# Weight pieces in one tile, block inverses on GpSimd, and a swap of two subtractions in a one-core hybrid encoder step

## The chip, the cores and the metric

The kernel runs on one core of a Trainium2 chip. A core has a matrix engine (PE, with its weight loads shown apart as PEld), a vector engine (DVE), a scalar engine (ACT), GpSimd (POOL) and a queue engine (SP, SyncE) from which this kernel issues all of its DMAs; 16 DMA engines move the bytes. Each engine takes its own instructions strictly in the order in which they stand in the program, and waits on semaphores for the others.

The metric is the device time of one execution in microseconds (us). Times below are of the kernel before, and one execution of it was taken by the profiler.

## The reference

One layer of a streaming encoder is computed, for a prompt of 2048 tokens and for 64 frames of a running stream ("sample"), width 1024, 16 heads of 64 in four groups of four heads.

- `proj = x @ w_in` gives the inputs of four mixers. A is a gated delta rule (a short convolution, then chunks with a triangular solve), B is stick-breaking attention, C is an mLSTM, D is HGRN2.
- Each head's output is normalised, two groups are gated, and `mix = o @ w_out`.
- `x = LN(alpha*x + mix)`, then `x = LN(alpha*x + relu(x@w1+b1)^2 @ w2 + b2)` with a hidden width of 4096.
- The new states and the new keys and values are outputs too.

Two places matter here. In mixer A a chunk of 128 tokens solves with `eye + lm`, unit lower triangular:

```python
sol = lax.linalg.triangular_solve(eye + lm, rhs, left_side=True, lower=True, unit_diagonal=True)
```

In mixer B the weight of a key is `exp(log_sigmoid(z) + after)`, where `after` sums `log_sigmoid(-z)` over all later keys up to the query. The kernel therefore walks the keys backward in steps of 128 keys and carries the running sum from step to step.

## The kernel before

**Numbers in two pieces.** PE multiplies rounded numbers (type fp32r), so an operand is split into a rounded part `hi` and a rest `lo = x - hi`. Every product is three matmuls (`mm3`): in L468 and L469 and L470 of the profile stand hi by hi, and the two mixed products. A split takes a copy that rounds (mostly ACT) and a subtraction (DVE or POOL).

**The dense work.** The tokens are in four blocks of 512, and the 64 sample tokens ride along. `project` multiplies each block by `w_in`, one column group after the other; `mix` multiplies by `w_out`; `mlp` does the two MLP products, and it begins for the first block when the fourth block is projected. In `mlp`, `up` makes 256 hidden columns (ReLU and square on ACT in L1632 and L1633, the rounded copy into `hh` on DVE in L1634, the rest on DVE in L1638), and `down` multiplies them by `w2` and adds to an accumulator `acc` on DVE (L1653).

**Weights.** `load_w` fetches one weight tile (128 x 512 or 528 numbers) for the matmuls. At a weight's first use SP loads it raw (L459), ACT makes `whi` (L460), POOL makes `wlo` (L461), and SP stores both to scratch in HBM (`wsp`, L196). At each later use SP loads both pieces from `wsp` by two DMAs of 256 KB (L196). Each piece has a ring of six tiles. SP waits at a load until the tile's last readers are done, and all DMAs behind it wait too.

**The other work.** Four generators run beside the dense one: attention (`attention`, then `attention_sample`), the gates, the delta rule (`gdn`) and the two memories (`mlstm`, `hgrn`). `interleave` places their PE work between the dense matmuls by due times; the order of PE's instructions is thus fixed when the program is written. The order on DVE, ACT, POOL and SP is made by the scheduler of the language, which simulates the program while it is built; a tile of a ring is given out there when a slot is free.

**The inverses.** `gdn` runs nine times (two chunks at a time for the prompt, one for the sample). It needs the inverse of the 16 x 16 diagonal blocks of all chunks and heads. They lie with one block per partition (64 partitions) in `ub`; L960 to L971 compute the inverse in `wb` row by row on DVE: a negation, and 15 times a product (L965, up to 15 x 15 numbers per partition) and a sum (L971). Then the inverses go through HBM (`wd`) to other partitions, and PE uses them (L1000 and on). All of L960 to L971 is one chain in which each instruction needs the one before.

**One attention step.** PE makes scores two steps ahead (L1358, L1359). `stick` bounds them (DVE L1323) and takes softplus (ACT L1288, L1289). `add_carry` adds the carry to one row (DVE L1298) and splits the result: ACT L1300 and the rest on POOL in L1301. PE sums over keys (L1308 with the rounded part, L1309 with the rest) into `c`. `weights` subtracts (DVE L1315), takes exp (ACT L1316), and splits: ACT L1318, and the rest on DVE in L1319. PE multiplies by the values (`add_up`: L1368 with the rounded part, L1369 with the rest), which stands on PE one step later, behind the sums of the next step. The carry of the next step comes from `c`. There are 160 such steps for the prompt and 17 for the sample.

Of the kernel before, what the change touches and what calls it, by code (L numbers as in the profile page):

```python
# [13 lines left out]
P = 128  # L14
D = 1024
# [15 lines left out]
R_AS, R_AR, R_AQ, R_AK, R_OB = 5, 4, 3, 6, 1  # L31
# [7 lines left out]
R_G2, R_G1, R_H2, R_H1 = 10, 9, 3, 12  # L39
# [17 lines left out]
def encoder_step(ctx: ExitStack, tc: tile.TileContext, a, o):  # L57
# [131 lines left out]
    pd = psring(psd, "d")  # L189

# [251 lines left out]
    def load_w(w, r0, k, c0, n, end=False):  # L442
# [129 lines left out]
    def into_place(b):  # L572

        ld = []
        for t in b.tiles:
            ld.append(bp.tile([P, 4 * UNIT], F32, tag="acc", name=nm("acc"), bufs=R_ACC)[:, :D])
            SP.dma_start(ld[-1][: t.n], t.x)
        if not b.i:
            yield 0, 4
        for j, t in enumerate(b.tiles):  # L580
            if b.i:
                yield from need("xfree", b.i, j)
            yield from put_T(t, t.off, [ld[j][:, 512 * g : 512 * g + 512] for g in range(2)])
# [284 lines left out]
    def gdn(u):  # L868
# [91 lines left out]
        DVE.tensor_scalar(ub[:PB], ub[:PB], -1.0, None, ALU.mult)  # L960
        fill_in(wb[:PB], 0.0)
        POOL.memset(wb[:PB].rearrange("p r c -> p (r c)")[:, ::17], 1.0)
        for i in range(14, -1, -1):
            m = 15 - i
            DVE.tensor_tensor(  # L965
                tb[:PB, :m, :m],
                wb[:PB, i + 1 :, i + 1 :].rearrange("p j c -> p c j"),
                ub[:PB, i, i + 1 :].unsqueeze(1).to_broadcast([PB, m, m]),
                ALU.mult,
            )  # L970
            DVE.tensor_reduce(wb[:PB, i, i + 1 :], tb[:PB, :m, :m], axis=AX.X, op=ALU.add)  # L971
# [320 lines left out]
    def add_carry(sp, carry):  # L1292
# [8 lines left out]
        POOL.tensor_tensor(sl, sp, sh.bitcast(F32), ALU.subtract)  # L1301
# [10 lines left out]
    def weights(zc, c):  # L1312
# [6 lines left out]
        DVE.tensor_tensor(al, zc, ah.bitcast(F32), ALU.subtract)  # L1319
# [175 lines left out]
    def bcast_row(src):  # L1495
        x = bp.tile([P, 4 * UNIT], F32, tag="brd", name=nm("brd"), bufs=R_BRD)[:, :D]
        SP.dma_start(x, src.partition_broadcast(P))
        return x
# [56 lines left out]
    def mix(ts_, ld):  # L1555

        for t in ts_:
            t.acc = bp.tile([P, 4 * UNIT], F32, tag="acc", name=nm("acc"), bufs=R_ACC)[: t.n, :D]
# [32 lines left out]
        for t in ts_:  # L1591
            POOL.tensor_tensor(t.acc, t.acc, bb1[: t.n], ALU.add)
            SP.dma_start(t.x1, t.acc)

# [244 lines left out]
```

## Time and profile before

| | us |
|---|---|
| runs (median of 3; lowest to highest) | 3465.78 (3459.81 to 3467.36) |
| the profiled execution, its own time | 3468.76 |
| its span, first to last instruction | 3466.7 |
| PE busy | 3160.0 (91%) |
| DVE busy | 2275.2 (66%) |
| ACT busy | 1342.0 (39%) |
| POOL busy | 860.7 (25%) |
| mean granted TensorE clock | 0.952 |

The page gives one execution. Busy times count instructions of the engine, not the waits of its sequencer, and not the issuing of DMAs. A row of a view by lines reads: line, engine, operation, output and inputs by the program's names, shape, count, then busy time and the mean of one, then the idle time of the engine just before these instructions and what ended it. The span of 3466.7 us and the own time of 3468.76 us differ by 2.06 us that lie around the instructions.

### The profile page before, as it was taken

How to read it: one execution, taken by the hardware profiler on the slowest of the kernel's cores; microseconds unless marked ns; L12 is line 12 of the kernel's file. 1: busy time of each engine (PE TensorE's matmuls, PEld its weight loads, DVE VectorE, ACT ScalarE, POOL GpSimd, SP SyncE). 2: the span in 40 equal slices, each digit the busy share in tenths (PEclk: the TensorE clock that was granted, in tenths of full speed). 3: DMA queues.
4: the chain of work that ended last, by engine and by line, in shares of the span. 5: the costliest groups of instructions: out<-in, count | busy, mean ns of one | idle time of the engine just before them, and what ended most of it. 6: DMA issues, size and time to landing. Idle time of an engine off the chain costs nothing.

```text
span 3466.7 us, 60038 instructions
## 1 busy us (share of the span) xinstructions
PE 3160.0 (91%) x20906; PEld 2686.4 (77%) x20906; DVE 2275.2 (66%) x5360; ACT 1342.0 (39%) x3048; POOL 860.7 (25%) x946
## 2 busy tenths in 40 slices
PE   6987799999889878988988987999999999999998
PEld 6977788878777667776766766888887888898987
DVE  2656556558757887888889889757556354564445
ACT  2433343425446346556556555444212111121111
POOL 3432112113124233455354453121101000010001
PEclk9998899999989889999988988999999999999999
DMA  7985666676567676665765875657787576765542
GB/s 236 304 267 177 185 213 187 201 212 196 175 207 232 202 250 191 204 220 189 249 223 187 268 204 167 197 163 240 247 279 261 187 265 235 263 228 161 167 159 88
DMA packets 573882, 735.62 MB, mean 212 GB/s; under 512 B 104472, under 2 KB 300748, under 8 KB 573580
## 3 DMA queue, kind: packets, MB, share of 16 engines
q1 hardware_dynamic: 573580, 731.79, 65.9%
q8 instruction: 166, 2.72, 0.3%
q14 instruction: 136, 1.11, 0.1%
HBM read 548.63 MB, written 182.94 MB: 211 GB/s over the span
## 4 chain that ended last, share of the span: by engine, by line
PE 43%; DVE 10%; DMA 2%; issue 1%; ACT 1%; SPq 1%; POOL 1%; POOLq 0%; DVEq 0%; ACTq 0%
PE d L468 13%; PE d L469 12%; PE d L470 12%; DVE acc L1653 1%; DVE g L890 1%; PE d L531 1%; DVE ar L1319 1%; DVE as L1315 0%; DVE g L965 0%; PE po L1369 0%; DVE as L1298 0%; PE a L1309 0%; SPq L196 0%; PE a L1358 0%; PE a L1308 0%
## 5 line engine op out<-in xcount | busy, mean ns | idle before, releaser
L468 PE MATMUL d<-XH,whi 128*128 128x512 f32 (+1 forms) x1840 | 678.6, 369 | 19.4 <-ACT whi L460 8.5
L469 PE MATMUL d<-XL,whi 128*128 128x512 f32 (+1 forms) x1840 | 662.1, 360 | 0.8 <-DVE XL L484 0.8
L470 PE MATMUL d<-XH,wlo 128*128 128x512 f32 (+1 forms) x1840 | 660.5, 359 | 1.2 <-DMA wlo<-wsp 0.7
L1653 DVE TENSOR_TENSOR acc<-d,acc 128x512 f32<-128x512 f32 x564 | 386.0, 687 | 251.5 <-PE d L470 239.3
L468 PE MATMUL d<-whi,hh 128*128 128x512 f32 x992 | 405.4, 409 | 8.0 <-ACT x L1632 2.8
L468 PEld LDWEIGHTS d<-XH,whi 128*128 128x128 f32 x1840 | 352.8, 192 | 69.2 <-ACT whi L460 8.7
L469 PE MATMUL d<-wlo,hh 128*128 128x512 f32 x992 | 397.7, 401 | 5.3 <-POOL wlo L461 5.2
L1301 POOL TENSOR_TENSOR ar<-as,ar 128x512 fp32r<-128x512 f32 (+3 forms) x177 | 210.0, 1186 | 753.5 <-ACT ar L1300 617.0
L470 PE MATMUL d<-whi,hh 128*128 128x512 f32 x992 | 396.6, 400 | 0.0
L470 PEld LDWEIGHTS d<-XH,wlo 128*128 128x128 f32 x1840 | 352.1, 191 | 53.4 <-DMA wlo<-wsp 1.1
L469 PEld LDWEIGHTS d<-XL,whi 128*128 128x128 f32 x1840 | 353.0, 192 | 45.6 <-DVE XL L484 1.5
L1632 ACT ACTIVATE x<-d,cbig 128x512 f32<-128x512 f32 (+1 forms) x160 | 97.8, 611 | 677.9 <-PE d L470 659.5
L461 POOL TENSOR_TENSOR wlo<-raw,whi 128x512 fp32r<-128x512 f32 (+1 forms) x204 | 276.2, 1365 | 299.4 <-ACT whi L460 199.7
L468 PE MATMUL d<-whi,XH 128*128 128x256 f32 (+1 forms) x1024 | 307.2, 300 | 15.9 <-DMA whi<-wsp 10.4
L469 PE MATMUL d<-wlo,XH 128*128 128x256 f32 (+1 forms) x1024 | 301.2, 294 | 17.9 <-DMA wlo<-wsp 11.0
L470 PE MATMUL d<-whi,XL 128*128 128x256 f32 (+1 forms) x1024 | 297.9, 291 | 1.2 <-DVE XL L484 1.1
L1634 DVE CAST hh<-x 128x512 fp32r<-128x512 f32 (+1 forms) x160 | 75.3, 471 | 272.3 <-ACT x L1633 272.1
L468 PEld LDWEIGHTS d<-whi,hh 128*128 128x128 f32 x992 | 190.6, 192 | 54.1 <-ACT x L1632 3.2
L469 PEld LDWEIGHTS d<-wlo,hh 128*128 128x128 f32 x992 | 190.9, 192 | 46.9 <-POOL wlo L461 5.5
L470 PEld LDWEIGHTS d<-whi,hh 128*128 128x128 f32 x992 | 190.5, 192 | 45.1
L469 PEld LDWEIGHTS d<-wlo,XH 128*128 128x128 f32 x1024 | 203.2, 198 | 23.8 <-DMA wlo<-wsp 14.7
L468 PEld LDWEIGHTS d<-whi,XH 128*128 128x128 f32 x1024 | 203.6, 199 | 22.5 <-DMA whi<-wsp 12.3
(439 smaller groups left out, 6352.2 us busy)
## 6 DMA issues: line engine op xcount, KB each, us to landing
whi<-wsp SPq DMA_DIRECT2D x644, 256.0 KB
wlo<-wsp SPq DMA_DIRECT2D x644, 256.0 KB
wsp<-whi SPq DMA_DIRECT2D x196, 256.0 KB
wsp<-wlo SPq DMA_DIRECT2D x196, 256.0 KB
raw<-in_w_dram SPq DMA_DIRECT2D x128, 256.0 KB
acc<-in_x_prompt_dram SPq DMA_DIRECT2D x32, 512.0 KB
raw<-in_w_in_dram SPq DMA_DIRECT2D x52, 256.0 KB
ak<-kk SPq DMA_DIRECT2D x80, 128.0 KB
```

The costliest lines, as they stand in the source:

```text
L461: POOL.tensor_tensor(lo, raw, hi.bitcast(F32), ALU.subtract)
L468: PE.matmul(out, lhsT=lh, rhs=rh, start=start, stop=False)
L469: PE.matmul(out, lhsT=lh, rhs=rl, start=False, stop=False)
L470: PE.matmul(out, lhsT=ll, rhs=rh, start=False, stop=stop)
L531: PE.matmul(pt, lhsT=lhs(k), rhs=r, start=k == ks[0] and i == 0, stop=k == ks[-1] and i == 1)
L890: DVE.scalar_tensor_tensor(dst[:, i], xin[:, i, j : j + N], convw(2 * p + i, j), dst[:, i], ALU.mult, ALU.add)
L1301: POOL.tensor_tensor(sl, sp, sh.bitcast(F32), ALU.subtract)
L1319: DVE.tensor_tensor(al, zc, ah.bitcast(F32), ALU.subtract)
L1632: ACT.activation(r, pt, AF.Relu, bias=b1c(ff))
L1634: DVE.tensor_copy(h[:, f, cs], r)
L1653: lambda pt, first, acc=acc: DVE.tensor_tensor(acc, pt, acc, ALU.add),
```

## The change

- **Weights.** `hi` and `lo` of a weight lie side by side in one tile `wt` with one ring of six, and in one scratch tensor. A first use stores both by one DMA, and a later use loads both by one DMA of 512 KB instead of two of 256 KB. Only the last 8 weights of the last MLP, whose pieces go into 16 tiles of other rings, are still fetched by two DMAs.
- **Inverses.** The negation on DVE goes. Column after column, for 15 columns, POOL now does a product and a subtraction of at most 64 numbers per partition, where DVE did a product and a sum.
- **Attention.** The rest in `add_carry` goes from POOL to DVE, and the rest in `weights` from DVE to POOL.
- **MLP.** The rounded copy into `hh` goes from DVE to ACT.
- **Tiles.** The accumulators (`acc`, 6), the broadcast rows (`brd`, 2) and the hidden tiles (`hh`, 2) are no longer rings whose slots the scheduler gives out: each is one fixed tile, cut into parts that the program takes by turn or from a list of free ones. Two rings get one tile less: `ak` (keys and values of attention, 6 to 5) and `g2` (tiles of `gdn`, 10 to 9).

PE's instructions and their order stay as they are, but for two neighbours that change places at the start.

```diff
-R_AS, R_AR, R_AQ, R_AK, R_OB = 5, 4, 3, 6, 1
+R_AS, R_AR, R_AQ, R_AK, R_OB = 5, 4, 3, 5, 1
...
-R_G2, R_G1, R_H2, R_H1 = 10, 9, 3, 12
+R_G2, R_G1, R_H2, R_H1 = 9, 9, 3, 12
...
+    accs = bp.tile([P, R_ACC, 4 * UNIT], F32, name="acc")
+    acc_free = list(range(R_ACC))
+
+    def acc_take(o):
+        o.acc_i = acc_free.pop(0)
+        o.acc = accs[: o.n, o.acc_i, :D]
+
+    def acc_give(o):
+        acc_free.append(o.acc_i)
+
+    brd_ = fixed("brd", 4 * UNIT, R_BRD)
+    hh_ = fixed("hh", -(-SB // P * 2 * BN // UNIT) * UNIT, R_HH, F32R)
...
-            hi, lo = (wp.tile([P, 2 * UNIT], F32R, tag=tag, name=nm(tag), bufs=W_SP)[:, :m] for tag in ("whi", "wlo"))
+            both = wp.tile([P, 4 * UNIT], F32R, tag="wt", name=nm("wt"), bufs=W_SP)[:, : 2 * m]
+            hi, lo = both[:, :m], both[:, m:]
         key = (w.tensor.name, r0, c0)
-        if key in split:
-            for x, d in zip((hi, lo), split[key]):
-                move(x, d)
-        else:
+        if key not in split:
...
-            split[key] = [dram([P, m], F32, "wsp") for _ in range(2)]
-            for x, d in zip((hi, lo), split[key]):
-                move(d, x)
+            split[key] = dram([P, 2 * m], F32, "wsp")
+            move(split[key], both)
+        elif end:
+            move(hi, split[key][:, :m])
+            move(lo, split[key][:, m:])
+        else:
+            move(both, split[key])
...
-        DVE.tensor_scalar(ub[:PB], ub[:PB], -1.0, None, ALU.mult)
         fill_in(wb[:PB], 0.0)
         POOL.memset(wb[:PB].rearrange("p r c -> p (r c)")[:, ::17], 1.0)
-        for i in range(14, -1, -1):
-            m = 15 - i
-            DVE.tensor_tensor(
-                tb[:PB, :m, :m],
-                wb[:PB, i + 1 :, i + 1 :].rearrange("p j c -> p c j"),
-                ub[:PB, i, i + 1 :].unsqueeze(1).to_broadcast([PB, m, m]),
-                ALU.mult,
-            )
-            DVE.tensor_reduce(wb[:PB, i, i + 1 :], tb[:PB, :m, :m], axis=AX.X, op=ALU.add)
+
+        for j in range(15, 0, -1):
+            up_ = [PB, j, 16 - j]
+            POOL.tensor_tensor(tb[:PB, :j, : 16 - j], bc(ub[:PB, :j, j], up_), wb[:PB, j, j:].unsqueeze(1).to_broadcast(up_), ALU.mult)
+            POOL.tensor_tensor(wb[:PB, :j, j:], wb[:PB, :j, j:], tb[:PB, :j, : 16 - j], ALU.subtract)
         DVE.tensor_copy(tb[:PB], wb[:PB].rearrange("p r c -> p c r"))
...
-        POOL.tensor_tensor(sl, sp, sh.bitcast(F32), ALU.subtract)
+        DVE.tensor_tensor(sl, sp, sh.bitcast(F32), ALU.subtract)
...
-        DVE.tensor_tensor(al, zc, ah.bitcast(F32), ALU.subtract)
+        POOL.tensor_tensor(al, zc, ah.bitcast(F32), ALU.subtract)
...
-                    DVE.tensor_copy(h[:, f, cs], r)
+                    ACT.copy(h[:, f, cs], r)
```

The order of the instructions shows three places. The line numbers of the changed kernel differ: there L483 is the raw load, L485 the rest of a weight, L222 the moves, L989 the last fill ahead of the inverse, L993 and L994 the inverse, L1321 the carry's row, L1324 the rest in `add_carry`, L1338 the subtraction in `weights`, L1342 the rest in `weights`.

POOL, at the fourth call of `gdn` (first chunks of the second block), before: L962 is the last fill ahead of the inverse, and L994 there is the masking that follows the inverse.

```order
L962 MEMSET g_2320_12363 64x16
L1138 TENSOR_TENSOR h_2343_12530<-h_2277_12164,cbig 128x256
L1301 TENSOR_TENSOR ar_12545<-as_12349,ar_12544 128x512
L200 MEMSET h_2357_12627 128x512
L200 MEMSET h_2359_12633 128x4
L994 TENSOR_TENSOR g_2324_12433<-g_2164_11518,cbig 64x256 x2
```

The same place on POOL in the changed kernel, cut in the fourth column of 15:

```order
L989 MEMSET g_2059_11918 64x16
L993 TENSOR_TENSOR g_2060_11919<-g_2058_11917,g_2059_11918 64x15
L994 TENSOR_TENSOR g_2059_11918<-g_2059_11918,g_2060_11919 64x15
L993 TENSOR_TENSOR g_2060_11919<-g_2058_11917,g_2059_11918 64x14x2
L994 TENSOR_TENSOR g_2059_11918<-g_2059_11918,g_2060_11919 64x14x2
L993 TENSOR_TENSOR g_2060_11919<-g_2058_11917,g_2059_11918 64x13x3
L994 TENSOR_TENSOR g_2059_11918<-g_2059_11918,g_2060_11919 64x13x3
L1161 TENSOR_TENSOR h_2078_12076<-h_2016_11719,cbig 128x256
L993 TENSOR_TENSOR g_2060_11919<-g_2058_11917,g_2059_11918 64x12x4
L1342 TENSOR_TENSOR ar_12086<-as_11769,ar_12085 128x512
```

Thirty instructions of the inverse now stand on POOL, and attention's rest of the weights (L1342) stands among them; 21 more of them follow before the next L1342.

DVE at the same call, before: the inverse (L960, L965, L971) stands among the steps of the memories (L1127 to L1132) and of attention (L1315, L1298, L1319).

```order
L960 TENSOR_SCALAR g_2319_12362<-g_2319_12362 64x256
L1127 COPY cbig<-h_12505 128x4
L965 TENSOR_TENSOR g_2321_12364<-g_2320_12363,g_2319_12362 64x1
L1128 SCALAR_TENSOR_TENSOR cbig<-cbig 128x4
L1315 TENSOR_TENSOR as_12214<-as_12214,a_12532 128x512
L1298 TENSOR_TENSOR as_12349<-as_12349,a_12532 1x512
L971 TENSOR_REDUCE g_2320_12363<-g_2321_12364 64x1
L1129 TENSOR_TENSOR cbig<-cbig 128x4
L965 TENSOR_TENSOR g_2321_12364<-g_2320_12363,g_2319_12362 64x2x2
```

The same attention step on DVE in the changed kernel:

```order
L1150 COPY cbig<-h_12051 128x4
L1151 SCALAR_TENSOR_TENSOR cbig<-cbig 128x4
L1338 TENSOR_TENSOR as_11769<-as_11769,a_12078 128x512
L1152 TENSOR_TENSOR cbig<-cbig 128x4
L1321 TENSOR_TENSOR as_11904<-as_11904,a_12078 1x512
L1153 RECIPROCAL cbig<-cbig 128x4
L1155 TENSOR_TENSOR h_2077_12062<-h_12051,cbig 128x256
L1157 TENSOR_TENSOR h_2077_12062<-h_2077_12062,h_2018_11724 128x256
L1324 TENSOR_TENSOR ar_12091<-as_11904,ar_12090 128x512
```

The inverse has left DVE, and the rest of the sums (L1324) stands where the rest of the weights (L1319) stood some rows later.

SP soon after the start, before: raw loads, stores of single pieces, and L1707, which clears scratch.

```order
L459 DMA raw_410<-in_w_in_dram 128x2x256
L196 DMA wsp_385<-wlo_379 128x512
L459 DMA raw_702<-in_w_in_dram 128x2x256
L196 DMA wsp_395<-wlo_389 128x512
L1707 DMA wd_370<-g_187_362 64x514
L459 DMA raw_712<-in_w_in_dram 128x2x256
L196 DMA wsp_405<-wlo_399 128x512
```

The same place on SP in the changed kernel:

```order
L483 DMA raw_403<-in_w_in_dram 128x2x256
L222 DMA wsp_386<-wt_381 128x1024
L483 DMA raw_683<-in_w_in_dram 128x2x256
L222 DMA wsp_393<-wt_388 128x1024
L483 DMA raw_690<-in_w_in_dram 128x2x256
L222 DMA wsp_400<-wt_395 128x1024
```

The three stores of `whi`, which stood further ahead, are gone into these. Over the whole program 1744 DMAs of single pieces become 872 of both.

More of the change, by code (lines that the diff above doesn't have):

```diff
@@ L189, in encoder_step, with fixed, f @@
     pd = psring(psd, "d")
+    def fixed(name, cols, n, dt=F32):
+        full = bp.tile([P, n * cols], dt, name=name)
+        turn = [0]
+        def f():
+            turn[0] += 1
+            i = (turn[0] - 1) % n
+            return full[:, i * cols : (i + 1) * cols]
+        return f
+    accs = bp.tile([P, R_ACC, 4 * UNIT], F32, name="acc")
[7 more added lines that the diff above has]
+    hh_ = fixed("hh", -(-SB // P * 2 * BN // UNIT) * UNIT, R_HH, F32R)
     def dram(shape, dt, s):
@@ L572, in into_place @@
     def into_place(b):
-        ld = []
         for t in b.tiles:
-            ld.append(bp.tile([P, 4 * UNIT], F32, tag="acc", name=nm("acc"), bufs=R_ACC)[:, :D])
-            SP.dma_start(ld[-1][: t.n], t.x)
+            acc_take(t)
+            SP.dma_start(t.acc, t.x)
         if not b.i:
@@ L582, in into_place @@
                 yield from need("xfree", b.i, j)
-            yield from put_T(t, t.off, [ld[j][:, 512 * g : 512 * g + 512] for g in range(2)])
+            yield from put_T(t, t.off, [t.acc[:, 512 * g : 512 * g + 512] for g in range(2)])
+            acc_give(t)
             if t.sample:
@@ L1557, in mix @@
         for t in ts_:
-            t.acc = bp.tile([P, 4 * UNIT], F32, tag="acc", name=nm("acc"), bufs=R_ACC)[: t.n, :D]
+            acc_take(t)
             SP.dma_start(t.acc, t.x)
@@ L1609, in residual @@
         for t in b.tiles:
-            t.acc = bp.tile([P, 4 * UNIT], F32, tag="acc", name=nm("acc"), bufs=R_ACC)[: t.n, :D]
+            acc_take(t)
             SP.dma_start(t.acc, t.x1)
```

6 lines of the change are left out of this document (4 added, 2 removed).

## The prediction

> **What bounds the kernel now.** I read the page first, then the windows of 200 us, then the waits of PE, and last the groups and single instructions that the change touches. From the page:
>
> ```profile
> span 3466.7 us, 60038 instructions
> ...
> PE 3160.0 (91%) x20906; PEld 2686.4 (77%) x20906; DVE 2275.2 (66%) x5360; ACT 1342.0 (39%) x3048; POOL 860.7 (25%) x946
> ...
> PE   6987799999889878988988987999999999999998
> ...
> PEclk9998899999989889999988988999999999999999
> ...
> PE 43%; DVE 10%; DMA 2%; issue 1%; ACT 1%; SPq 1%; POOL 1%; POOLq 0%; DVEq 0%; ACTq 0%
> ```
>
> PE is the bound: it is busy for 91%, and idle for 306.7 us. The idle time and the lower clock lie in the first two thirds (the first 27 of 40 slices). The last line, the shares of the chain of waits, puts DVE next, far ahead of the DMAs, ACT and POOL. The windows say where this happens; the columns are the length, busy PE, PEld, DVE, ACT and POOL with counts, the granted clock, the DMA share and GB/s:
>
> ```profile
> 1100.00:1300.00 200.00, 160.16 (x1018) 130.42 (x1017) 166.04 (x420) 88.16 (x195) 63.58 (x60) 0.87 0.71 233
> 1300.00:1500.00 200.00, 177.11 (x1166) 148.94 (x1165) 167.18 (x375) 114.11 (x254) 85.28 (x85) 0.92 0.63 203
> 1500.00:1700.00 200.00, 180.52 (x1318) 144.62 (x1317) 170.17 (x352) 123.65 (x279) 95.88 (x97) 0.95 0.64 208
> 1700.00:1900.00 200.00, 169.34 (x1251) 136.29 (x1250) 177.03 (x392) 116.23 (x267) 101.41 (x97) 0.90 0.67 216
> 1900.00:2100.00 200.00, 174.59 (x1100) 137.88 (x1099) 173.46 (x370) 109.80 (x240) 94.22 (x94) 0.94 0.72 221
> 2300.00:2500.00 200.00, 199.06 (x988) 160.66 (x987) 120.59 (x223) 79.08 (x153) 28.14 (x26) 1.00 0.70 229
> ```
>
> Once attention is nearly over (2300 to 2500) PE is busy for 199 of 200 us at clock 1.00, and nothing that another engine gives up can help there. From 1100 to 2100 PE is idle for 138.3 of 1000 us, and DVE is busy for 853.9. An idle PE also lowers the clock: its mean there is 0.916, so of the 861.7 busy us 72 are lost, 0.52 per idle us. I therefore multiply each us of idle time taken away or added by 1.5, an estimate from these rows.
>
> Whom PE waits for (total, times, longest):
>
> ```profile
> PE po L1369 <- DVE ar L1319: 19.9, 12, 3.4
> PE a L1309 <- POOL ar L1301: 17.7, 17, 2.4
> PE m L1051 <- DVE g L1047: 15.5, 6, 9.5
> PE d L468 <- ACT whi L460: 14.1, 5, 8.5
> PE h L1118 <- DMA h<-mlq: 13.8, 1, 13.8
> PE d L469 <- POOL wlo L461: 11.9, 7, 5.2
> PE m L1000 <- DMA g<-wd: 11.8, 2, 8.5
> PE d L468 <- DMA whi<-wsp: 11.6, 9, 3.7
> PE d L469 <- DMA wlo<-wsp: 11.3, 17, 2.5
> PE h L1242 <- DVE h L1219: 10.5, 3, 5.3
> PE m L933 <- DVE g L918: 8.6, 3, 3.4
> PE d L468 <- DVE as L1323: 6.7, 2, 5.4
> ```
>
> These twelve sum to 153.4 us; DVE's five are 61.2 of them (40%), the DMAs' four 48.5. No single wait is large, so the change works on many small ones.
>
> The change is summed against the profiled execution's own 3468.76 us, which is 2.98 above the median.
>
> **Weights in one DMA.** What SP spends per issue (ns, minimum, median, maximum), and what it waits for:
>
> ```profile
> L196 SPq DMA_DIRECT2D whi<-wsp x668: 314/349/1554, 299.9 to 3405.3; - x167
> L196 SPq DMA_DIRECT2D wlo<-wsp x668: 319/383/1872, 301.1 to 3405.8; - x167
> ...
> SPq L196 <- PE d L470: 693.8, 360, 9.4
> ```
>
> 872 DMAs go, at some 0.38 us about 330 us of SP's time. The bytes stay. SP mostly waits for free tiles (693.8 us), so it isn't full on average; it is crowded only where many loads come together, and there `mlq`, `wd` and the keys stand behind the weights. Against this, 256 KB take 1.1 us at the 233 GB/s of a window, so `hi` may land up to 1.1 us later when it comes with `lo`: 9 waits, up to +10. The gain lies between 0 and the DMAs' whole 48.5 us, times 1.5. I take a quarter, by choice, because the later `hi` eats into it: 12 us, **−18** with the clock (bounds +15 and −73).
>
> The Trainium skill ("DMA: Bandwidth & Descriptors", section "Issuing engines are not separate DMA queues") says that the time to initiate a DMA is usually small relative to the DMA itself. By it this term would be about nothing and the sum 18 us higher, 3441. Here 0.38 us stand beside 1.1 us of transfer, a third, which is not small.
>
> **Inverses and casts off DVE.** The groups (busy, mean ns, idle time before them), and the negation:
>
> ```profile
> L965 DVE TENSOR_TENSOR g<-g,g 64x1 f32<-64x1 f32 (+9 forms) x135 | 53.2, 394 | 2.6
> L971 DVE TENSOR_REDUCE g<-g 64x1 f32<-64x1 f32 (+9 forms) x135 | 30.6, 227 | 2.4
> L1634 DVE CAST hh<-x 128x512 fp32r<-128x512 f32 (+1 forms) x160 | 75.3, 471 | 272.3 <-ACT x L1633 272.1
> ...
> L960 DVE TENSOR_SCALAR g<-g x9: 256/285/823, 271.4 to 2238.3; 64x256 f32<-64x256 f32 x8, 16x256 f32<-16x256 f32 x1
> L1632 ACT ACTIVATE x<-d,cbig x160: 484/675/692, 1380.0 to 3424.3; 128x512 f32<-128x512 f32 x96, 128x288 f32<-128x288 f32 x64
> ```
>
> The inverses cost DVE 53.2 + 30.6 + 9 × 0.285 = 86.4 us, spread over nine calls from 271 to 2238; of the casts' 75.3 us the part in 1100 to 2100 is (2100 − 1380) / (3424 − 1380) = 35%. Relief in that stretch: 86.4 × 1000 / 1967 = 44, and 26.5.
>
> What POOL now pays has no row. The nearest two-input operations on POOL, and an instance of such an operation beside DVE:
>
> ```profile
> L311 POOL TENSOR_TENSOR g<-g,cbig 32x32 f32<-32x32 f32 x1 | 0.2, 242 | 0.0
> L1208 POOL TENSOR_TENSOR h<-h,h 128x128 f32<-128x128 f32 (+1 forms) x50 | 25.1, 501 | 0.0
> ...
> 1621.62 0.16 DVE L226 TENSOR_SCALAR cbig<-cbig 128x4 f32<-128x4 f32 x1
> 1632.92 2.54 POOL L461 TENSOR_TENSOR wlo<-raw,whi 128x512 fp32r<-128x512 f32 x2 [0.37 <-ACT whi L460]
> 1633.30 0.94 DVE L226 TENSOR_SCALAR cbig<-cbig 128x4 f32<-128x4 f32 x1
> ```
>
> From 32 to 128 numbers per partition the price rises by 2.7 ns each; an operation of the inverse has j(16 − j) numbers, 45 on average, so 242 + 13 × 2.7 = 277 ns (bounds 242 and 501). A call is 30 × 0.28 = 8.4 us, against 9.6 on DVE: the chain is about as long as before, and `wd` no later. POOL gets 270 × 0.28 = 76 us more. The last three rows show that DVE pays for POOL's work: the same little operation took 0.16 us alone and 0.94 beside it, 0.78 of POOL's 2.54. By that third, 25 of the 76 us come back on DVE (bounds 0 and 76), 13 of them in the stretch.
>
> So DVE's relief there is 44 + 26.5 − 13 = 58, its free time goes from 146 to 204 us, and I let waits on DVE shrink as its free time grows, by 28% (a choice, with the relief evenly spread): 138.3 × 0.40 × 0.28 = 15, and 23 with the clock. Elsewhere DVE gets some 79 us on 1046 free ones, 7.5% of 168 × 0.40, with the clock 8. Term: **−30**. Bounds: 0, if the waits pass to ACT or POOL, and −83, if all of DVE's share in the stretch goes.
>
> **The swap.** The two rests (shapes apart), and one rest with its matmul:
>
> ```profile
> L1301 POOL TENSOR_TENSOR ar<-as,ar 128x512 fp32r<-128x512 f32 x112 | 159.4, 1423 | 466.7 <-ACT ar L1300 370.5 <-PE d L470 16.1 <-DVE acc L1612 10.6
> L1319 DVE TENSOR_TENSOR ar<-as,ar 128x512 fp32r<-128x512 f32 x112 | 95.0, 848 | 11.2 <-ACT ar L1318 10.7
> ...
> 1602.86 0.68 DVE L1319 TENSOR_TENSOR ar<-as,ar 128x512 fp32r<-128x512 f32 x1
> 1606.76 0.39 PE L1369 MATMUL po<-ar,ak 128*128 128x512 f32 x1
> ```
>
> The engines trade equal counts, so busy times stay. The sums' rest is ready 1423 − 848 = 0.58 us earlier: 17 waits, −10. The weights' rest comes as much later: 12 waits, +7. It also joins POOL's in-order queue, behind the inverse's 30 operations and `wlo`; its slack is about 3 us, as in the last two rows, and I put +8 on what exceeds it. Term: **+5**, bounds −20 and the rival's +126 below.
>
> **At nothing.** ACT gets the 160 casts (75 us): it is the engine that feeds DVE's rest of `hh` anyway, and in the MLP's late part it is busy for 79 of 200 us; without that cover, a cast of half a us delays a matmul. The fixed tiles and the two shorter rings change when slots come free; no row prices them: −5 to +15.
>
> **Sum:** 3468.76 − 18 − 30 + 5 = 3425.8, which on the median is 2.98 less, **3423**.
>
> **The rivals.**
>
> *Nothing comes of it.* PE's waits are many and small; when one releaser is faster, the next may be as late, and the scheduler's new order shuffles them. For it: no wait above 20 us. Against: DVE's 85% over 1000 us. About 3462, the median less a few us.
>
> *More.* DVE is the real bound of the stretch, and its whole share goes: −83 instead of −30, so 3370. For it: the chain's 10%; against: the casts are only a third inside it.
>
> *Slower: the weights' rests queue on POOL.* In POOL's new order 18 of the 177 rests stand behind operations of the inverse, counted there as 30, 30, 26, 22, 20, 20, 18, 18, 12, 12, 12, 12, 10, 10, 6, 6, 4 and 2. If a whole run stands ahead of each and an operation costs L1208's 0.5 us, the runs take 1 to 15 us, 84 us in all beyond a slack of 3, times 1.5 is 126; with −18, −30, −10 and +7 that is 3541 on the median. At 0.35 us it is 46, so +69 and 3484. It decides from 34 us, at 0.30 us per operation with whole runs ahead; if a rest arrives mid-run on average, even 0.5 us gives only 22 us, and no loss. For it: POOL's queue is in order, and 0.30 is close to my 0.28. Against: the order is made by simulated readiness, so most of a run should be done when the rest comes.
>
> The Trainium skill ("GPSIMD Engine Reference", section "4.1 Engine selection") speaks against this move: elementwise work belongs on VectorE, and GpSimd is about 2 times slower with two inputs. At twice L965's mean an operation would cost 0.8 us, beyond the point where this rival decides. The traces bear the rule out for large tiles only in part (1423 against 848 ns, 1.7), and for small ones not (242 ns for the only such row).
>
> *The change doesn't do it.* PE still waits for the ACT half and the POOL half of a first-use weight apart, and the DMA count falls as said; I give this nothing.
>
> **How the numbers follow.** What a measurement can tell from no change is about 0.2%, 7 us here: 3459 to 3473. Forecast (3390 to 3455) 0.55; more (around 3370) 0.13; nothing (3455 to 3475) 0.16; slower (3473 to 3541) 0.16. Faster: 0.55 + 0.13 + 0.03 of nothing; same 0.11; slower 0.16 + 0.02. The range from 3370 to 3490 leaves out half of "more" and some 0.09 of "slower".
>
> **What would show it.** Right: DVE's busy time falls by 130 to 160 us, `g` operations on POOL take 0.24 to 0.3 us, the idle PE time from 1100 to 2100 falls from 138 to about 115, and its clock rises. The waits of L469 on its own DMA go and those of L468 grow a little. Wrong: PE's waits on POOL for the weights' rest beyond 60 us (slower), operations of the inverse over 0.35 us, DVE's operations stretched beside POOL by more than the 76 us, or the same idle PE time with other releasers (nothing).

## The result and the profile after

| | before | after |
|---|---|---|
| runs, median (lowest to highest), us | 3466.57 (3459.81 to 3467.43) | 3438.53 (3434.30 to 3442.32) |
| the profiled execution, its own time | 3468.76 | 3434.30 |

The ratio is 0.9925, with a 95% interval of 0.9908 to 0.9943: 28 us (0.75%) faster by the medians, 34 us between the two profiled executions. The forecast was 3423, 43 us faster, with a range of 3370 to 3490.

From the page of the changed kernel:

```profile
span 3432.6 us, 58736 instructions
...
PE 3156.8 (92%) x20906; PEld 2689.8 (78%) x20906; DVE 2162.0 (63%) x4921; ACT 1423.0 (41%) x3208; POOL 926.5 (27%) x1216
```

PE's idle time (span less busy) went from 306.7 to 275.8 us, so 31 of the 34 us are idle time, and only 3 are shorter matmuls. Between these two traces an idle us costs 1.1 us, where 1.5 was estimated; the granted clock from 1100 to 2100, which was to rise, stays at 0.92. DVE lost 113 us of busy time, where 130 to 160 were expected. The windows of the changed kernel, with the same columns as before:

```profile
1100.00:1300.00 200.00, 163.47 (x1128) 135.94 (x1127) 166.77 (x403) 90.03 (x200) 69.71 (x91) 0.91 0.69 232
1300.00:1500.00 200.00, 180.28 (x1123) 149.22 (x1121) 163.68 (x342) 121.44 (x270) 103.01 (x124) 0.93 0.67 218
1500.00:1700.00 200.00, 181.76 (x1300) 146.44 (x1301) 163.91 (x335) 124.51 (x274) 87.03 (x100) 0.93 0.62 204
1700.00:1900.00 200.00, 170.82 (x1267) 135.76 (x1266) 174.84 (x358) 126.22 (x285) 103.69 (x110) 0.93 0.67 219
1900.00:2100.00 200.00, 171.24 (x1251) 137.30 (x1251) 176.20 (x368) 114.35 (x255) 102.07 (x126) 0.90 0.64 213
```

DVE's busy time in these 1000 us fell from 853.9 only to 845.4, not to 796, and PE's idle time from 138.3 to 132.4, not to 115. DVE is as full as it was, and the stretch has become shorter instead. Since PE's instructions have the same order in both kernels, the two traces can be laid side by side instruction by instruction. How much earlier the changed kernel starts the same PE instruction:

| time in the kernel before, us | 200 | 300 | 700 | 1200 | 1500 | 2200 | 3400 |
|---|---|---|---|---|---|---|---|
| lead of the changed kernel, us | 2.9 | 20.1 | 5.9 | 5.5 | 21.1 | 36.2 | 34.2 |

There are two gains: 17 us between 200 and 300, most of it given back by 700, and 31 us between 1200 and 2200. Whom PE waits for now:

```profile
PE d L496 <- DMA wt<-wsp: 36.9, 19, 6.7
PE a L1332 <- DVE ar L1324: 33.2, 25, 4.2
...
PE d L497 <- POOL wt L485: 7.7, 6, 3.8
...
PE po L1392 <- POOL ar L1342: 7.2, 3, 5.2
...
PE po L1501 <- POOL ar L1342: 3.4, 5, 1.3
```

Three things contradict the prediction at once. The wait on a weight's DMA is 36.9 us, where the two pieces cost 11.6 + 11.3. The wait on the sums' rest, which was to shrink by 10, rose from 17.7 to 33.2. The wait on the weights' rest, which was to grow, fell from 19.9 to 7.2 (L1392). The wait on `h<-mlq` (13.8 us, ending at 295 us) is gone, which makes most of the early gain. The price of the inverse's operations was right, 297 and 289 ns for the forecast 277:

```profile
L993 POOL TENSOR_TENSOR g<-g,g 64x15 f32<-64x15 f32 (+9 forms) x135 | 40.0, 297 | 37.5 <-DMA g<-ud 23.3 <-DMA x<-o 5.7
L994 POOL TENSOR_TENSOR g<-g,g 64x15 f32<-64x15 f32 (+9 forms) x135 | 39.1, 289 | 9.4
```

### The profile page after: what moved, and what is told of

Read it like the earlier page. It is cut to its first block, busy times and chain, and to the rows that moved or that the text cites. A ratio compares the mean times of both kernels' runs of the same rounds, so it can differ in the third digit from the quotient of the medians.

```text
span 3432.6 us, 58736 instructions
## 1 busy us (share of the span) xinstructions
PE 3156.8 (92%) x20906; PEld 2689.8 (78%) x20906; DVE 2162.0 (63%) x4921; ACT 1423.0 (41%) x3208; POOL 926.5 (27%) x1216
## 4 chain that ended last, share of the span: by engine, by line
PE 58%; DVE 16%; DMA 14%; SPq 3%; issue 3%; ACT 3%; POOL 2%; POOLq 0%; DVEq 0%; ACTq 0%
PE d L496 16%; PE d L497 16%; PE d L498 16%; DMA wt<-wsp 3%; SPq L222 1%; DVE g L918 1%; DMA raw<-in_w_in_dram 1%; DMA vv<-x 1%; PE d L559 1%; DVE ar L1324 1%; DVE acc L1677 1%; DMA ga<-x 1%; DMA h<-r_M 1%; DVE as L1321 1%; DVE acc L1600 1%
## 5 line engine op out<-in xcount | busy, mean ns | idle before, releaser
L496 PE MATMUL d<-XH,wt 128*128 128x512 f32 (+1 forms) x1840 | 675.9, 367 | 9.3 <-DVE acc L1600 4.4
L498 PE MATMUL d<-XH,wt 128*128 128x512 f32 (+1 forms) x1840 | 659.3, 358 | 2.4 <-POOL wt L485 2.4
L497 PE MATMUL d<-XL,wt 128*128 128x512 f32 (+1 forms) x1840 | 661.0, 359 | 0.0
L496 PE MATMUL d<-wt,hh 128*128 128x512 f32 x992 | 404.7, 408 | 11.3 <-DVE acc L1677 6.0
L496 PEld LDWEIGHTS d<-XH,wt 128*128 128x128 f32 x1840 | 352.2, 191 | 59.2 <-DVE acc L1600 5.3
L498 PE MATMUL d<-wt,hh 128*128 128x512 f32 x992 | 397.6, 401 | 0.0
L497 PE MATMUL d<-wt,hh 128*128 128x512 f32 x992 | 396.5, 400 | 0.0
L498 PEld LDWEIGHTS d<-XH,wt 128*128 128x128 f32 x1840 | 350.1, 190 | 54.8 <-POOL wt L485 3.1
L1342 POOL TENSOR_TENSOR ar<-as,ar 128x512 fp32r<-128x512 f32 (+3 forms) x177 | 202.3, 1143 | 699.4 <-ACT ar L1341 487.8
L497 PEld LDWEIGHTS d<-XL,wt 128*128 128x128 f32 x1840 | 350.7, 191 | 44.5 <-DVE XL L512 0.4
L485 POOL TENSOR_TENSOR wt<-raw,wt 128x512 fp32r<-128x512 f32 (+1 forms) x204 | 275.3, 1358 | 294.6 <-ACT wt L484 203.1
L496 PE MATMUL d<-wt,XH 128*128 128x256 f32 (+1 forms) x1024 | 313.2, 306 | 43.2 <-DMA wt<-wsp 33.2
L497 PE MATMUL d<-wt,XH 128*128 128x256 f32 (+1 forms) x1024 | 303.9, 297 | 8.1 <-POOL wt L485 7.7
L498 PE MATMUL d<-wt,XL 128*128 128x256 f32 (+1 forms) x1024 | 301.6, 295 | 1.2 <-DVE XL L512 1.2
L496 PEld LDWEIGHTS d<-wt,XH 128*128 128x128 f32 x1024 | 207.6, 203 | 51.4 <-DMA wt<-wsp 37.5
L496 PEld LDWEIGHTS d<-wt,hh 128*128 128x128 f32 x992 | 190.5, 192 | 55.9 <-DVE acc L1677 6.7
L498 PEld LDWEIGHTS d<-wt,hh 128*128 128x128 f32 x992 | 190.0, 192 | 44.6
L497 PEld LDWEIGHTS d<-wt,hh 128*128 128x128 f32 x992 | 190.5, 192 | 41.7
L497 PEld LDWEIGHTS d<-wt,XH 128*128 128x128 f32 x1024 | 207.9, 203 | 10.7 <-POOL wt L485 9.4
```

The source lines that it names most:

```text
L485: POOL.tensor_tensor(lo, raw, hi.bitcast(F32), ALU.subtract)
L496: PE.matmul(out, lhsT=lh, rhs=rh, start=start, stop=False)
L497: PE.matmul(out, lhsT=lh, rhs=rl, start=False, stop=False)
L498: PE.matmul(out, lhsT=ll, rhs=rh, start=False, stop=stop)
L1342: POOL.tensor_tensor(al, zc, ah.bitcast(F32), ALU.subtract)
```

## The experiments

The kernels of one call ran on one chip, beside the kernel before, and each ratio is to that. Most have the rings `ak` at 4 and `g2` at 8 tiles, so that they share one base. A ratio of 0.001 is 3.5 us, and half an interval is 0.0011 to 0.0024, so a difference of two ratios is uncertain by some 6 to 11 us.

### First call: a base, and one part undone at a time

`short_rings`, the changed kernel with

```diff
-R_AS, R_AR, R_AQ, R_AK, R_OB = 5, 4, 3, 5, 1
+R_AS, R_AR, R_AQ, R_AK, R_OB = 5, 4, 3, 4, 1
-R_G2, R_G1, R_H2, R_H1 = 9, 9, 3, 12
+R_G2, R_G1, R_H2, R_H1 = 8, 9, 3, 12
```

> The changed kernel with two rings one tile shorter still (ak 5 to 4, g2 9 to 8); it is the base that the next three are held against. Sum theory (each part of the change is worth its term, rings nothing): 3438, as the changed kernel, within 5. Order theory (any edit makes the scheduler shuffle the other engines, and the time goes up and down by 10 to 15 us with that, whatever the edit is): anywhere from 3425 to 3455.

Measured: 3438.21 us, ratio 0.9900 (0.9880 to 0.9921). It is 0.0025 below the changed kernel's, on another chip: shorter rings cost nothing that can be told. Both theories allow it. The order theory is not refuted by the later runs either, for differences under its 10 to 15 us.

`no_weights`, on that base, with two tiles and two DMAs per weight again:

```diff
-            both = wp.tile([P, 4 * UNIT], F32R, tag="wt", name=nm("wt"), bufs=W_SP)[:, : 2 * m]
-            hi, lo = both[:, :m], both[:, m:]
+            hi, lo = (wp.tile([P, 2 * UNIT], F32R, tag=tag, name=nm(tag), bufs=W_SP)[:, :m] for tag in ("whi", "wlo"))
```

> As short_rings, but hi and lo in two tiles with two DMAs again. Sum theory: 18 us slower than short_rings. Early theory (20 us of the gain come from one transfer before 300 us, the rest of the change sums to little): 20 us slower, with the PE wait on h<-mlq of some 14 us back before 300 us. Order theory: within 15 us of short_rings, either sign, and no such wait.

Measured: 3447.14 us, 0.9922 (0.9901 to 0.9943), 8 us slower than the base by the ratios, which is within the uncertainty of 10. PE waits for `h<-mlq` only 1.9 us in it, so the early theory falls: the long wait doesn't hang on the number of weight DMAs.

`no_inverse`, on that base, with the old loop on DVE (L960 to L971 of the kernel before) in place of the new one on GpSimd:

```diff
-        for j in range(15, 0, -1):
-            up_ = [PB, j, 16 - j]
...
+        for i in range(14, -1, -1):
+            m = 15 - i
...
```

> As short_rings, but the inverses on DVE again. Sum theory: DVE busy 65 us more, POOL 79 less, and 16 us slower than short_rings, lost between 1100 and 2100 us. Early theory: within 5 us. Order theory: within 15 us, either sign.

Measured: 3466.43 us, 0.9978 (0.9964 to 0.9993), 27 us slower than the base, more than any of the three theories had. It is the largest part. By the two traces laid side by side, 13 us of it are lost by 1100 us already, ahead of the stretch that the sum theory named. Its busy row stands under that of the base:

```profile
PE 3154.8 (92%) x20906; PEld 2689.7 (78%) x20906; DVE 2162.0 (63%) x4921; ACT 1424.6 (41%) x3208; POOL 922.4 (27%) x1216
```

```profile
PE 3160.0 (91%) x20906; PEld 2692.1 (78%) x20906; DVE 2199.3 (63%) x5200; ACT 1421.5 (41%) x3208; POOL 859.3 (25%) x946
```

DVE has 279 instructions more, which the kernel before priced at 86 us, but is busy for only 37 us more. So 49 us, not 25, of what the move took off DVE come back as DVE's other operations beside GpSimd's. The relief, 37 us, is little over half of the 61 (86 less 25) that the prediction reckoned with, and yet the gain is about twice the inverse's part of the term.

`no_swap`, on that base:

```diff
-        DVE.tensor_tensor(sl, sp, sh.bitcast(F32), ALU.subtract)
+        POOL.tensor_tensor(sl, sp, sh.bitcast(F32), ALU.subtract)
...
-        POOL.tensor_tensor(al, zc, ah.bitcast(F32), ALU.subtract)
+        DVE.tensor_tensor(al, zc, ah.bitcast(F32), ALU.subtract)
```

> As short_rings, but attention's two rests on their old engines. Sum theory as the prediction had it: 5 us faster than short_rings. The other way round (the wait of PE on the weights' rest fell from 19.9 to 10.6 us with the swap, that on the sums' rest rose from 17.7 to 33.2): PE waits 33 us less for L1324's successor and 9 more for the other, so 5 to 10 us faster. Order theory: within 15 us, either sign.

Measured: 3459.57 us, 0.9957 (0.9943 to 0.9971), 20 us slower than the base. The swap gains, and none of the three theories said so. PE's wait of 11.9 us on `h<-mlq` is back here.

### Second call: none of the parts, one alone, and the rests put together

`none_of_four`: fixed tiles and the base's rings, with the weights, inverses, rests and cast as before (its edits are those above, and the cast back on DVE).

> Fixed tiles and short_rings' rings, but weights in two tiles, inverses on DVE, the rests and the cast on their old engines: what the tiles and rings do by themselves. Additive theory (the parts' effects add: 9 of the weights, 28 of the inverses, 21 of the swap, and short_rings is 1.0% below the kernel before, 35 us): the tiles and rings with the cast cost about 23, so this kernel is 15 to 25 us slower than the kernel before. Overlap theory (the parts clear the same waits, so the last one removed shows more than its share): this kernel is within 7 us of the kernel before.

Measured: 3471.65 us, 1.0011 (0.9999 to 1.0023). The tiles and rings are worth nothing that can be told, as predicted. The three removals sum to 55 us, though the base is only 38 below this kernel, so the parts overlap: each, when it alone is removed, brings back more than its share.

`cast_alone`, on `none_of_four`:

```diff
-                    DVE.tensor_copy(h[:, f, cs], r)
+                    ACT.copy(h[:, f, cs], r)
```

> none_of_four with the cast into hh on ACT. Prediction's term: 14 us faster than none_of_four (75 us of DVE's time, a third of it where DVE is full). Cover theory (most casts come after attention, when PE waits for nothing; what remains delays ACT's roundings for attention): within 6 us of none_of_four.

Measured: 3459.03 us, 0.9980 (0.9969 to 0.9991), 11 us faster than `none_of_four`, uncertain by 6. DVE is busy for 77 us less (2180.7 for 2257.9), all that the casts took, and laid side by side it gains 12.5 us between 1500 and 2200, where casts fall into the busy stretch, after 4 us lost ahead of it. So relief of DVE seems to pay here, at about the size of the term; that the order of the other engines did it isn't excluded.

`both_on_gpsimd`, on `short_rings`:

```diff
-        DVE.tensor_tensor(sl, sp, sh.bitcast(F32), ALU.subtract)
+        POOL.tensor_tensor(sl, sp, sh.bitcast(F32), ALU.subtract)
```

> As short_rings, but both rests of attention on GpSimd: DVE loses about 130 us of work, GpSimd gains some 200. Relief theory (DVE's fullness is the bound, so work off it is what gains): faster than no_swap, which has only the weights' rest more on DVE, by 10 to 30 us, and not slower than short_rings. Chain theory (the sums' rest stands in the chain from one attention step to the next, the weights' rest doesn't; what counts is that the quick engine makes the former): 15 to 40 us slower than short_rings, no faster than no_swap.

`both_on_vector`, on `short_rings`:

```diff
-        POOL.tensor_tensor(al, zc, ah.bitcast(F32), ALU.subtract)
+        DVE.tensor_tensor(al, zc, ah.bitcast(F32), ALU.subtract)
```

> As short_rings, but both rests on DVE: about 120 us more on DVE, 200 fewer on GpSimd. Relief theory: 20 to 50 us slower than short_rings. Chain theory: the sums' rest stays on the quick engine, so within 10 us of short_rings, a little slower by DVE's queue. A third one, contention (a subtraction on GpSimd stretches DVE's own operations, so that it saves DVE little): DVE busy rises by less than 90 us, and the time stays within 10 us.

Measured: 3471.79 us, 1.0015 (1.0003 to 1.0026), and 3433.36 us, 0.9890 (0.9872 to 0.9907). With the first call, which ran on another chip, they make a square:

| ratio to the kernel before | weights' rest on DVE | weights' rest on GpSimd |
|---|---|---|
| sums' rest on DVE | 0.9890 | 0.9900 |
| sums' rest on GpSimd | 0.9957 | 1.0015 |

The sums' rest matters most: on DVE it is 23 and 40 us better. With it there, the engine of the weights' rest makes no difference that can be told; with both on GpSimd it is 20 us worse. The relief theory falls, since the kernel with the least work on DVE is the slowest. The busy rows, first of both on GpSimd, then of both on DVE:

```profile
PE 3165.9 (91%) x20906; PEld 2697.1 (78%) x20906; DVE 2097.3 (60%) x4744; ACT 1423.8 (41%) x3208; POOL 1094.0 (32%) x1393
```

```profile
PE 3153.7 (92%) x20906; PEld 2688.9 (78%) x20906; DVE 2174.2 (63%) x5098; ACT 1422.6 (41%) x3208; POOL 734.5 (21%) x1039
```

Against the base's 2162.0, DVE in the second does 177 subtractions more and is busy for only 12 us more, though these take 118 us by themselves:

```profile
L1342 DVE TENSOR_TENSOR ar<-as,ar 128x512 fp32r<-128x512 f32 (+3 forms) x177 | 117.9, 666 | 46.9 <-ACT ar L1341 46.0
```

The other three sides of the square give more relief. In `no_swap` DVE's row is

```profile
PE 3147.6 (91%) x20906; PEld 2680.6 (78%) x20906; DVE 2144.5 (62%) x4921; ACT 1425.0 (41%) x3208; POOL 928.1 (27%) x1216
```

so the sums' rests, 120 us on DVE in `both_on_vector`, free 30 us when they alone leave it; from `short_rings` to both on GpSimd it is 65 us for 128, and from `no_swap` 47 for 136. The third theory, contention, thus has its two signs, and it shows in single operations too: in `short_rings` a two-input DVE operation of 128 x 4 (TENSOR_TENSOR `cbig<-cbig`) takes 160 ns on average with nothing beside it on GpSimd, and 473 ns with something there. A subtraction of this size on GpSimd costs DVE, in its other operations, between half and nine tenths of what doing it would. That this decides the time isn't shown.

The chain theory gets its order of times right, but not its reason. The mean time from the end of the rounded copy to the end of the sums' rest is 0.31 + 1.19 = 1.50 us in the kernel before, on GpSimd, and 1.12 + 0.74 = 1.86 in the changed one: DVE is quicker, but the rest waits 1.12 us in its queue. The rest is ready later on DVE, as PE's longer wait (33.2 us) says, and the kernel is faster all the same. The weights' rest, on the other hand, is ready sooner on GpSimd (1.50 us for 1.94). But with both on GpSimd the two are ready after 1.82 and 1.46 us, with both on DVE after 1.84 and 1.76, and the first is the slower kernel by 43 us.

### Third call: the transfer that PE waited for, and the inverse's chain

The wait of 12 to 14 us on `h<-mlq` is in the traces of the kernel before, of `no_swap`, `none_of_four`, `cast_alone` and `both_on_vector` (and of `weights_alone` below), where the weights' rests are on DVE, and in none where they are on GpSimd. `first_twelve`, on `both_on_vector`:

```diff
-        DVE.tensor_tensor(al, zc, ah.bitcast(F32), ALU.subtract)
+        uid.append(0)
+        E = POOL if len(uid) <= 13 else DVE
+        E.tensor_tensor(al, zc, ah.bitcast(F32), ALU.subtract)
```

> both_on_vector with the first 12 of the 177 weights' rests on GpSimd. In its order of SP the load of h<-mlq that PE waited 12 to 14 us for stands ahead of the stores of the inverses (wd), as in the changed kernel; in both_on_vector it stands behind them. Place theory (the wait of 12 to 14 us, and the 14 us by which the profiles part before 300 us, come from that place alone): no PE wait on h<-mlq over 3 us, and 14 us faster than both_on_vector, so 1.4 to 1.6% faster than the kernel before. Absorbed theory (what is lost before 300 us is made up by 2400 us, since other waits shrink): within 5 us of both_on_vector, 1.1%.

`first_eight`, the same with `len(uid) <= 9`:

> The control of first_twelve: only the first 8 rests on GpSimd, and the load stands behind the stores again. Place theory: the wait of 12 to 14 us is there, and the time is within 5 us of both_on_vector (1.1% faster than the kernel before). If instead the rests' engine at the start matters by itself: about two thirds of what first_twelve gains.

SP's issues in `first_eight` (start, duration, and the count at the end of the row), and its PE wait (total, times, longest):

```profile
285.18 2.14 SPq L1002 DMA_DIRECT2D wd<-g  x6
288.36 1.58 SPq L1002 DMA_DIRECT2D wd<-g  x4
290.95 1.58 SPq L1002 DMA_DIRECT2D wd<-g  x4
...
293.75 1.26 SPq L1111 DMA_DIRECT2D h<-mlq  x2
```

```profile
PE h L1141 <- DMA h<-mlq: 15.7, 2, 13.3
```

and the same in `first_twelve`:

```profile
272.21 1.26 SPq L1111 DMA_DIRECT2D h<-mlq  x2
284.63 1.02 SPq L1002 DMA_DIRECT2D wd<-g  x3
```

In the one the load stands on SP behind the stores of the inverses, which wait for DVE and GpSimd; in the other it stands ahead, is issued 21 us sooner, and PE doesn't wait for it at all. Four rests on another engine were enough to turn the scheduler's order. Measured: 3433.39 us, 0.9874 (0.9852 to 0.9896), and 3440.39 us, 0.9896 (0.9877 to 0.9914). The place of the load is shown; its worth of 14 us is not. The ratios differ by 8 us, which is within the uncertainty, and the profiled spans by 6. Of the lead of 11 us that `first_twelve` has over `both_on_vector` at 400, 3 are left at the end; of its 15 over its own control, `first_eight`, 4 at 1200 and 7 at the end. The absorbed theory fits better.

`first_twelve` has the lowest ratio of all; `short_rings` and `both_on_vector` can't be told from it.

`idle_inverse`, the changed kernel with `g2` at 8, and the old 30 instructions besides the new ones, on the same input, their results read by nobody:

```diff
+        junk = g1([P, 16, 16])
+        for i in range(14, -1, -1):
+            m = 15 - i
+            DVE.tensor_tensor(
+                junk[:PB, :m, :m],
+                ub[:PB, i + 1 :, i + 1 :].rearrange("p j c -> p c j"),
...
+            DVE.tensor_reduce(junk[:PB, 15, 1 : 1 + m], junk[:PB, :m, :m], axis=AX.X, op=ALU.add)
```

> The changed kernel with g2 one tile shorter, inverses on GpSimd, and besides them DVE does its old 30 instructions per call once more on the same input into a tile that nobody reads, so DVE keeps the old work but no step of PE's path stands in it. Relief theory (what the inverses' move gained is DVE's time): DVE busy 80 us more, and 20 to 28 us slower than the changed kernel, as no_inverse is. Chain theory (it gained because a chain of 30 dependent steps no longer waits its turn on a full DVE; on DVE two calls took 45 us from first to last, on GpSimd 14 and 24): GpSimd's calls stay at 10 to 24 us, and the time is within 10 us of the changed kernel.

Measured: 3541.96 us, 1.0189 (1.0165 to 1.0213), 100 us slower than `short_rings` by the ratios: neither theory's number. The experiment didn't do what it was meant to. Its fifth call, first on DVE, then on GpSimd:

```profile
1234.99 0.15 DVE L993 TENSOR_TENSOR g<-g 64x1 f32<-64x1 f32 x1 [1.05 <-DMA g<-ud]
...
1283.31 0.38 DVE L999 TENSOR_REDUCE g<-g 64x15 f32<-64x225 f32 x1
```

```profile
1280.46 2.35 POOL L1624 TENSOR_TENSOR acc<-acc,brd 128x1024 f32<-128x1024 f32 x1 [5.25 <-DVE acc L1621]
1282.76 0.55 POOL L1002 TENSOR_TENSOR g<-g,g 64x15 f32<-64x15 f32 x1
```

PE's longest wait in it:

```profile
PE m L1032 <- DMA g<-wd: 81.4, 12, 28.2
```

GpSimd's chain stands in its queue behind other work and starts only when DVE's idle chain is all but over, 48 us late. So the inverses come later by the whole of DVE's chain, and PE waits 81.4 us for them. It measures something else: what a late inverse costs. The time from the first to the last step of the nine calls, summed, beside the ratio:

| kernel | first to last step, sum of nine, us | ratio |
|---|---|---|
| `short_rings` (GpSimd) | 148 | 0.9900 |
| `no_inverse` (DVE) | 203 | 0.9978 |
| `idle_inverse` (DVE, then GpSimd) | 375 | 1.0189 |

From the first to the second it is 27 us of time for 56 of chain, 0.48 per us; to the third 100 us for 227, 0.44. By DVE's busy time the same steps would be 0.7 (27 for 37) and 1.6 (100 for 62). Over the whole program one line fits the length of the chain, and none DVE's load.

Cut at 1200 us, ahead of the fifth call, the line is gone. Laid side by side (one trace each), `no_inverse` is by then 16.7 us behind `short_rings`, though its first four calls took 51 us and those of `short_rings` 55; `idle_inverse` is 17.2 behind, though its four took 93. From there on the two lose 9 and 90 us for 59 and 189 us of longer chain, 0.16 and 0.48 per us. Up to 1200 they have lost the same, and what they have in common is the 30 instructions per call on DVE: there the relief theory fits better, or a shuffled order.

One wait shows the chain itself. At the first use of the fifth call's inverses PE waits 8.5 to 11.2 us in all five kernels that have them on DVE alone (the kernel before, `none_of_four`, `cast_alone`, `weights_alone`, `no_inverse`), where this call takes 44 to 48 us, and never over 1 us in the eight that have them on GpSimd alone, where it takes 13 to 15. In `no_inverse`:

```profile
PE m L1028 <- DMA g<-wd: 10.2, 1, 10.2
```

So a late inverse does cost PE time, at this one place, though 4 of these 10 us are left 60 us later (16.6 us behind at 1250, 20.9 at 1350). How the 27 us divide between the chain, DVE's load and the order isn't shown.

`weights_alone`, `none_of_four` with the weights' tile and DMA of the changed kernel (the diff of `no_weights` backward):

> none_of_four with both pieces of a weight in one tile and one DMA. Prediction's term: 18 us faster than none_of_four. The other measurement (no_weights against short_rings, 9 us with an uncertainty of as much): 5 to 10 us faster. By the skill's rule as the prediction read it: none.

Measured: 3478.45 us, 1.0008 (0.9994 to 1.0023), beside 1.0011 for `none_of_four`: no gain. PE's waits for the weights' DMAs, first of `none_of_four`, then of `weights_alone`:

```profile
PE d L494 <- DMA whi<-wsp: 15.1, 10, 3.6
...
PE d L495 <- DMA wlo<-wsp: 8.8, 13, 2.1
...
PE d L496 <- DMA wlo<-wsp: 6.5, 1, 6.5
```

```profile
PE d L496 <- DMA wt<-wsp: 32.0, 18, 4.2
```

30.4 us became 32.0; between `no_weights` and `short_rings` 37.0 became 25.8, so no sign holds for both pairs. What SP waits for, in `none_of_four` and in `weights_alone` (693.8 in the kernel before, 793.4 in the changed one):

```profile
SPq L222 <- PE d L496: 682.3, 357, 9.2
```

```profile
SPq L222 <- PE d L498: 820.8, 413, 11.0
```

Summed over the two traces, SP spends 1627 and 1296 us on issuing DMAs, and 1783 and 2089 on waiting. Of the 331 us that it no longer spends on issuing, it waits 306, and 138 of them in these two rows, for the same tiles to come free.

## Why the prediction was right, and where not

The direction and the range were right; 28 us for 43 is two thirds of it. But the sum came out near in part by luck: the weights' gain was put too high by some 10 to 18 us and the swap's too low by 25, and the parts don't add.

- **The weights' DMAs, −18.** Mis-sized: 8 us by `no_weights`, uncertain by 10, and nothing by `weights_alone`, uncertain by 7. The step that failed is "I take a quarter" of the DMAs' waits. Nearly all of the issuing time saved became waiting, so a shorter queue hardly issues a load sooner, and `hi` now lands with `lo`. The wait on `h<-mlq` was counted as SP's crowding; it was the place of one load in SP's order. The Trainium skill ("DMA: Bandwidth & Descriptors", section "Issuing engines are not separate DMA queues") has the time to initiate a DMA as usually small relative to the DMA. By it the term is about nothing, which is what `weights_alone` measured, and the prediction set it aside.
- **Inverses, in the term of −30.** The price per operation was right, and "the chain is about as long as before" was wrong. It added the durations, 9.6 us on DVE and 8.4 on GpSimd. On DVE each step waited behind whatever stood in between. The fifth call in the kernel before:

```profile
1226.33 0.16 DVE L965 TENSOR_TENSOR g<-g,g 64x16 f32<-64x16 f32 x1
1226.42 0.15 DVE L229 TENSOR_SCALAR cbig<-cbig 128x4 f32<-128x4 f32 x1
1226.48 1.16 DVE L1148 SCALAR_TENSOR_TENSOR cbig<-cbig,h,h 64x65 f32<-64x65 f32 x4
1227.68 0.42 DVE L1315 TENSOR_TENSOR as<-as,a 128x256 f32<-128x256 f32 x1
1228.13 0.41 DVE L1298 TENSOR_TENSOR as<-as,a 1x256 f32<-1x256 f32 x1
1228.58 0.16 DVE L971 TENSOR_REDUCE g<-g 64x4 f32<-64x16 f32 x1
```

  and in the changed kernel on GpSimd:

```profile
1216.07 0.21 POOL L993 TENSOR_TENSOR g<-g,g 64x15 f32<-64x15 f32 x1 [5.68 <-DMA x<-o]
1216.37 0.24 POOL L994 TENSOR_TENSOR g<-g,g 64x15 f32<-64x15 f32 x1
1216.68 0.23 POOL L993 TENSOR_TENSOR g<-g,g 64x28 f32<-64x28 f32 x1
1216.99 0.25 POOL L994 TENSOR_TENSOR g<-g,g 64x28 f32<-64x28 f32 x1
```

  On DVE 2.1 us lie between a product and its sum of 0.16 us; on GpSimd the steps follow every 0.31 us. From first to last this call took 45.5 us before and 13.5 after, the nine together 209 and 139. The prediction put nothing on that; PE waits 8.5 us for this call's inverses before, and not after. The relief of DVE, by which the prediction reckoned, was 37 us for 61. The 27 us that `no_inverse` lost are twice what the relief was to bring; which share of them the chain has stays open.
- **The cast, in the same term.** 75 us off DVE, and 11 us faster by itself, uncertain by 6, in the stretch that was named. Right as far as can be told.
- **The give-back.** 25 us were set down, with 76 as the bound; 49 were measured. It is one reason why DVE is nearly as full as before.
- **The swap, +5.** Wrong in sign: 20 us faster. It compared the durations (1423 and 848 ns) and left out the wait in DVE's queue, so both readings of PE's waits came out the wrong way round. That an earlier rest isn't what decides is shown by the kernel with both on GpSimd; what does is not.
- **Fixed tiles and rings, 0.** Right: 1.0011.
- **"Slower".** PE's waits for the weights' rest are 7.2 and 3.4 us, far from 60. The inverse's operations took 0.29 us, just under the 0.30 from which this rival decides with whole runs ahead, and the rests began 0.35 us on average after their rounded copy, so they were hardly held up.

What stays open is why the sums' rest on GpSimd costs 23 to 40 us. One observation goes with it: the subtraction in `weights` on DVE begins on average 1.54 to 1.72 us after the sums' last matmul in the six traces with that rest on GpSimd, and 1.23 to 1.40 in seven of the eight with it on DVE; but in the eighth, `no_weights`, it is 1.61, and that kernel is not slower than `short_rings` by anything that can be told. The rests also share GpSimd with the inverses, whose nine calls take 182 us there with both rests, and 121 with none; yet PE waits for `wd` in neither. Whether contention or the scheduler's order decides wasn't tried.

## What to carry to other kernels

A chain of small dependent steps takes its steps times the wait for a turn, not the sum of its durations: on a full in-order engine look at the time from its first to its last instruction (45.5 us here for 9.6 of work); an engine that has gaps can be through sooner, even at the same price per step. What that is worth is read from the bound engine's waits. A rate that fits the totals of three kernels is weak evidence: cut the traces at one time and see whether it holds on both sides. Work off a full engine pays only as far as the other engine doesn't slow it down, so compare the busy time of the whole engine and not that of the moved lines, and in more than one pair of kernels. Where a scheduler makes the order, four moved instructions can move a transfer by 20 us; lay the traces side by side by the engine whose order is fixed before a wait that has gone is credited to the edit.

## What the hardware showed that was not expected

- Moving subtractions of 128 x 512 to GpSimd (1.1 to 1.4 us each there) relieves DVE of a part only: of 118 to 136 us of its own time for 177 of them, its busy time falls by 12 to 65 us on the four sides of the square. The Trainium skill ("GPSIMD Engine Reference", section "1. Specifications") has GpSimd's interfaces to SBUF as shared with VectorE, with contention with DVE instructions that have two SBUF inputs or run in a 2-port mode; the slowed 128 x 4 operation, with two inputs, agrees (160 and 473 ns).
- At small sizes GpSimd is close to DVE. A product of 64 numbers per partition took 0.33 us on GpSimd in the changed kernel (median) and 0.26 on DVE in the kernel before; one of 15 took 0.21 on GpSimd, one of 16 took 0.17 on DVE. The Trainium skill ("GPSIMD Engine Reference", section "4.1 Engine selection") has a factor of about 2 for two inputs; here it is 1.2 to 1.3.
- What a us of idle PE costs can't be read from one pair of traces: 1.1 us between the two profiles, and against `short_rings` from 0.7 (`no_swap`) to 1.5 (`both_on_gpsimd`), while `no_weights` is 13 us longer with the same idle time.
